# Pieces of 256 columns for POOL's subtractions, gates as scalar operands, one copy moved to VectorE, q transposed a step ahead, three idle products

## The chip, the cores and the metric

The kernel runs on one core of one Trainium2 chip. The metric is device time in microseconds (us) of one execution; the time before is the median of three runs. Beside that median stands one execution recorded by the hardware profiler, whose rows are shown below. The engines are TensorE (PE, with its weight load as PEld), VectorE (DVE), ScalarE (ACT), GpSimd (POOL) and SyncE (SP), whose queue issues the DMA transfers.

## The reference

A trunk of two layers over 256 tokens of width 1024, in f32. Cut to its core:

```
for i in range(2):
    proj = x @ w_in[i]                        # one input projection
    mix  = nsa_mixer(...) if i == 0 else mla_mixer(...)   # 12 heads of 64
    xa   = memory_cross_attention(xq, mk, mv)             # 4 heads, 256 memory tokens
    y    = concat([mix, xa]) @ w_out[i]
    x    = layer_norm(alpha * x + y)
    x    = layer_norm(alpha * x + hier_moe(x))   # top group of 4, top 2 of its 4 experts
```

The mixer of layer 0 (`nsa_mixer`) has three branches for each head, each weighted by a sigmoid gate of its own and then added:

```
o = gb[..., 0:1] * o_c + gb[..., 1:2] * o_s + gb[..., 2:3] * o_w
```

`o_c` attends to compressed keys and values (blocks of 32 tokens through a small network), `o_s` to the selected blocks of 64 tokens, `o_w` to a window of 512, which with 256 tokens is plain causal attention. 12 query heads share 4 heads of keys and values. The mixer of layer 1 is latent attention with low-rank queries and keys.

## The kernel before

**Precision.** An f32 value is kept as two rounded halves, `h` (a cast) and `l` (the value minus the cast), and a product is three matmuls: h times h, l times h, h times l. `split` (L354 to L380) does this for a weight tile that has landed in the arena of SBUF, in two halves: the cast on ACT (L369) or DVE (L371), the subtraction on POOL (L378), in some places on DVE. `piece` (L811 to L818) does the same for a quarter of the output projection (cast L815, subtraction L816).

**Stages.** Cross attention's keys and values and the projections of layer 0 come first, to about 100 us, interleaved with attention from about 50 us; its attention lasts to about 175 us, the output projection and layer norm to 195 us. The experts of layer 0 run from 200 to 411 us, in eight pairs; the attention of layer 1 to about 505 us, its experts to about 716 us. The weights stream through one queue of SP (L239). A plan lists the loads in order; `pump` issues the next one as soon as the arena has a slot for it.

**The attention of layer 0** is a list of 14 steps of two heads each: steps 0 and 1 are cross attention, 2 to 4 the selected branch of the first half of the heads, 5 to 7 its window branch, 8 to 10 and 11 to 13 the same for the second half. `attention` (L716 to L757) writes the order by hand. While step j is being finished, step j+1 has begun: its scores on PE (L647, with the causal mask at L652), then the transposes of step j's probabilities (L696), the row maxima of j+1 on DVE (L663), the exponentials on ACT (L669, their sums come out beside them), and for each head pair on DVE the copy of the transposed probabilities out of PSUM (L705) and `factors`: reciprocal of the sums (L674), times the gate (L676). `norm` multiplies the probabilities by these factors on ACT (L684). `pv` (L713) is the product with the values.

```
def factors(self, i):
    sm = self.sm[i]
    V.reciprocal(sm, sm)
    if self.gates:
        V.tensor_tensor(sm, sm, self.gates(i), op=OP.mult)
```

Work of other kinds is put between by three means: `extra(j, late)` (from L1279) runs named work at step j, `pull(FILLS[j])` takes so much from a queue of generators, and `need(name)` drains that queue up to a name. `g_qT(kp, r)` (L1046 to L1059) transposes a pair of query heads on PE (L1051), casts the two halves on ACT (L1055) and subtracts on DVE (L1058); step 8 + r reads what `g_qT(1, r)` writes, with r = 0 coming from the queue. `v_done` (L1029 to L1032) copies projected values out of PSUM on ACT (L1031); of `vw`, the window branch's, this comes within step 6's extra work. `g_sc` (L1152) is the compressed branch's scores and `g_pc` the transposes (L1176) and copies (L1177) of its probabilities (pcT). In layer 1's attention, L905 is the last step of the layer norm, L555 the low half of a transposed x.

**Banks.** PSUM is handed out in eight banks that rotate: a product into a new bank waits until the one who read that bank last is done. `warm(n)` (L481) issues n products on constants, whose result nobody reads, into a bank of its own.

Of the kernel before, what the change touches and what calls it, by code (L numbers as in the profile page):

```python
# [10 lines left out]
F32 = mybir.dt.float32  # L11
# [4 lines left out]
OP = mybir.AluOpType  # L16
# [3 lines left out]
P = 128  # L20
S = 256
D = 1024
NT = S // P
# [18 lines left out]
FILLS = [6.0, 2.0, 3.0, 3.0, 3.0, 3.0, 3.0, 3.0, 1.6, 1.6, 1.6, 0.0, 1.6, 1.6]  # L42
# [66 lines left out]
def trunk(ctx: ExitStack, tc: tile.TileContext, A, out, dbg=None, layers=2, kb=ARENA_KB):  # L109
    nc = tc.nc  # L110
    PE, V, SC, G = nc.tensor, nc.vector, nc.scalar, nc.gpsimd
# [45 lines left out]
    def spare_room(nm, side, n):  # L157
        rp = open_pool(nm, side)
        return Arena(rp.tile([P, n * UNIT], F32, name=nm), n * UNIT)

    def open_ring(l):

        spare_for[:] = [c + str(l) for c in "gud"]
        if not extra_room:
            pools["qk"].close()
        pools["ring"].close()
        spare.append(spare_room("ring", "right", 2 if extra_room else 3))
        pump()
# [83 lines left out]
    def done(*keys):  # L252
        for k in keys:
            home(k).drop(k)
        pump()
# [95 lines left out]

    splits, parts = {}, {}

    def split(key, hi=None, lo=None):  # L354

        if key in splits:
            return
        if key not in parts:
            t = get(key)
            a, n = t.shape[1], t.shape[2]  # L360
            for ring_ in (WH, WL):
                ring_.append(ring_.pop(0))
            parts[key] = (t, a) + tuple(r[0][:, :a * n].rearrange("p (a b) -> p a b", a=a) for r in (WH, WL))
        t, a, wh, wl = parts[key]
        hi, lo = hi or ((SC, SC) if key in ("kc", "vc", "vs") else (V, SC)), lo or (G, G)
        for j in range(2):
            c = slice(j * a // 2, (j + 1) * a // 2)
            if hi[j] is SC:
                SC.copy(wh[:, c, :], t[:, c, :])  # L369
            elif hi[j]:  # L370
                hi[j].tensor_copy(wh[:, c, :], t[:, c, :])  # L371
        if lo[0] is None:
            return
        for j in range(2):
            c = slice(j * a // 2, (j + 1) * a // 2)
            if lo[j] is None:
                return
            lo[j].tensor_tensor(wl[:, c, :], t[:, c, :], wh[:, c, :].bitcast(F32), op=OP.subtract)  # L378
        splits[key] = (wh, wl)
        done(key)  # L380

# [95 lines left out]
    def warm(n):  # L477

        b = bank("warm")
        for _ in range(n):  # L480
            PE.matmul(b, onesb, onesb[:, None, :].to_broadcast([P, 4, P]), start=True, stop=True)  # L481
# [57 lines left out]
    def run(g):  # L539
        for _ in g:  # L540
            pass
# [90 lines left out]
    class Step:  # L632
# [39 lines left out]
        def factors(self, i):  # L672
            sm = self.sm[i]
            V.reciprocal(sm, sm)  # L674
            if self.gates:
                V.tensor_tensor(sm, sm, self.gates(i), op=OP.mult)  # L676

        def norm(self, i):
            n0, sm = self.n0, self.sm[i]
# [33 lines left out]
                PE.matmul(o[i * 64:(i + 1) * 64, q0:S], vget(i, k), pTs[i][:, a:a + S - q0],  # L713
                          start=first and k == 0, stop=False, skip_group_check=True)

    def attention(steps, fills, extra, prologue, last=lambda: None):  # L716


        steps[0].scores()
        steps[0].softmax_a()  # L720
        for i in range(2):
            steps[0].exps(i)
        for i in range(2):
            steps[0].factors(i)
            steps[0].norm(i)
        pull(prologue)
        for j, st in enumerate(steps):
            nx = steps[j + 1] if j + 1 < len(steps) else None
            if nx is not None:
                nx.scores()  # L730
            else:
                last()
            st.transposes()
            if nx is not None:
                nx.softmax_a()
                nx.exps(0)
                if nx.act:
                    nx.exps(1)
                    for i in range(2):
                        st.evac(i, V)  # L740
                        nx.factors(i)
                    for i in range(2):
                        nx.norm(i)
                else:
                    st.evac(0, V)
                    st.evac(1, SC)
                    nx.factors(0)
                    nx.norm(0)
                    nx.exps(1)
                    nx.factors(1)  # L750
                    nx.norm(1)
            else:
                st.evac(0, V)
                st.evac(1, SC)
            extra(j, 0)
            pull(fills[j])
            st.oget(st)  # L757
            extra(j, 1)
# [51 lines left out]
    def piece(l, h, part, q, hi, lo):  # L810

        key = "wo%d_%d%s" % (l, h, part)
        t = get(key)[:, 2 * q:2 * q + 2, :]
        wh, wl = splits[key, q] = [r[:, q * 1024:(q + 1) * 1024].rearrange("p (c f) -> p c f", c=2) for r in W0]
        (hi.copy if hi is SC else hi.tensor_copy)(wh, t)  # L815
        lo.tensor_tensor(wl, t, wh.bitcast(F32), op=OP.subtract)  # L816
        if q:
            done(key)  # L818

# [114 lines left out]
    def nsa():  # L934
        tmp = ar.temp

        v_sb = {"vw": tmp("vw_sb", [P, NT, 256])}
# [90 lines left out]

        def v_done(name):  # L1029
            def f(pa):  # L1030
                SC.copy(v_sb[name], pa.rearrange("p (t c) -> p t c", t=NT))  # L1031
            return f  # L1032

        def q_done(pas):
# [12 lines left out]
        def g_qT(kp, r):  # L1047

            pt = bank()
            for t in range(NT):  # L1050
                PE.transpose(pt[:, t * P:(t + 1) * P],  # L1051
                             q_tm[:, t, 2 * r:2 * r + 2, :].rearrange("p h d -> p (h d)"), ident)
            for i in range(2):
                q, v = qS[kp][2 * r + i], pt[i * 64:(i + 1) * 64, :S]
                SC.copy(q[0:64, :], v)  # L1055
            for i in range(2):
                q, v = qS[kp][2 * r + i], pt[i * 64:(i + 1) * 64, :S]
                V.tensor_tensor(q[64:P, :], v, q[0:64, :].bitcast(F32), op=OP.subtract)  # L1058
            yield 0.21  # L1059
# [192 lines left out]
        def branch_steps(b, kp, kname, vname, first, deps):  # L1252
            res = []
            for r in range(3):
                p_ = kp * 3 + r

                def fin(s_, r=r, p_=p_):
# [16 lines left out]
        steps = (cross_steps(0, xqT, obx)  # L1274
                 + branch_steps(1, 0, "ks", "vs", True, lambda: (need("ksT", "qT0"), pull(1.3))) + branch_steps(2, 0, "kw", "vw", False, kw_ready)
                 + branch_steps(1, 1, "ks", "vs", True, lambda: need("qT1")) + branch_steps(2, 1, "kw", "vw", False, None))
# [3 lines left out]
        def extra(j, late):  # L1280
            if not late:

                if j == 1:
                    run(g_qT(0, 1))
                    run(g_qT(0, 2))
                if j == 5:
                    run(g_kT("ks", 1))
                if j == 6:
                    need("vw")
                    open_ring(0)  # L1290
                if j == 7:
                    run(g_qT(1, 1))
                if j == 8:
                    run(g_qT(1, 2))
                    ar.drop("ks_tm", "okx", "q_tm")
                    pump()
                if j == 9:
                    run(g_kT("kw", 1))
                    ar.drop("kw_tm")
                    pump()  # L1300
                if j == 11:
                    run(g_pc(1))
                    q_("pv1", g_cmp_pv(1))
                if j in (9, 10):
                    next(sc1[0])
                return
            if j == 8:
                sc1.append(g_sc(1))
            if j in (8, 9):
                next(sc1[0])  # L1310
            if 5 <= j < 5 + 4:
                next(prep)
            if j == 10:
                need("o0a")
                piece(0, 1, "a", 0, SC, G)
                piece(0, 1, "a", 1, SC, G)
                pump()
            if j == 12:
                need("pv1")
                ar.drop("vs_sb", "vblk0", "vblk1", "pcT0", "pcT1", "sc")  # L1320
                pump()
            if j == 1:
                SC.copy(okx, obx[0])
                ring_close("px", "pTx")
                ar.drop("mkT0", "mv0_sb", "xqT")
                ar.set_top(12.5)
                pump()
            if j == 6:
                need("vw")
                evac_o(okx, 6)  # L1330
            if j == 7:
                need("pv0")
                q_("o0a", g_out(0, 0))
            if j == 7:
                evac_o(ob[0], 0)
            if j == 8:
                evac_o(ob[1], 2, 1)

        pull(2.0)
        ring_open(*CROSS)  # L1340
        attention(steps, FILLS, extra, 3.0, lambda: first_pieces(0))
        need("pv1")
        evac_o(ob[2], 3)
        evac_o(ob[3], 5, 1)
# [3 lines left out]
    def first_pieces(l):  # L1348
        for t in range(NT):
            g_piece(l, 1, "a", 0, t)  # L1350
# [751 lines left out]
```

## Time and profile before

| | us |
|---|---|
| three runs | 736.11, 736.69, 737.65 |
| median | 736.69 |
| profiled execution | 737.44 |
| its span | 735.7 |
| PE busy | 702.9 (96%) |
| DVE busy | 290.5 (39%) |
| ACT busy | 217.3 (30%) |
| POOL busy | 146.6 (20%) |

The span runs from the first instruction to the last; 1.74 us of the profiled execution lie around it. Busy shares are means over stages with different limits: PE is busy nearly all the time in the experts' stages and less in the attention stages. POOL's work lies almost wholly before 200 us and in layer 1's attention.

### The profile page before, as it was taken

The numbers are of one execution on the slowest core, as the hardware profiler recorded it, in microseconds if no ns is written. First come the engines' busy times: TensorE is split into PE (matmuls) and PEld (weight loads), VectorE is DVE, ScalarE is ACT, GpSimd is POOL, SyncE is SP. The second block draws the span as 40 slices with busy tenths as digits, with TensorE's granted clock in tenths as the row PEclk, the third lists the DMA queues.
The fourth block names the chain that finished last, engine by engine and source line by source line (L and its number), as shares of the span: only waits on it lengthen the run. The fifth ranks groups of instructions, "written<-read, shape, count | busy, mean of one in ns | idle before, by whom it ended". The sixth has DMA issues, their size and how long they took to land. (4 is left out here: it accounts for less than half of the span.)

```text
span 735.7 us, 10761 instructions
## 1 busy us (share of the span) xinstructions
PE 702.9 (96%) x4119; PEld 418.9 (57%) x4119; DVE 290.5 (39%) x706; ACT 217.3 (30%) x527; POOL 146.6 (20%) x164
## 2 busy tenths in 40 slices
PE   7999998889999999999998999999999999999993
PEld 6999897767643534435344587777435335344342
DVE  4367686763640311121010767646512112111106
ACT  4454457573320301101001465443213001011011
POOL 5887444030210400000000450021203000000003
PEclk9999999789999999999999999999999999999997
DMA  9895865427698999999999995457879999999971
GB/s 294 256 281 163 302 247 175 192 72 269 233 342 329 419 352 421 419 419 418 420 419 380 385 395 212 156 223 290 343 303 420 418 419 418 421 418 419 421 264 58
DMA packets 66727, 235.57 MB, mean 320 GB/s; under 512 B 10923, under 2 KB 30446, under 8 KB 47214
## 3 DMA queue, kind: packets, MB, share of 16 engines
q1 hardware_dynamic: 66670, 234.82, 82.9%
q8 instruction: 34, 0.56, 0.3%
q14 instruction: 23, 0.19, 0.1%
HBM read 233.76 MB, written 1.05 MB: 319 GB/s over the span
## 5 line engine op out<-in xcount | busy, mean ns | idle before, releaser
L1772 PE MATMUL yb<-arena 128*64 128x512 f32 x328 | 88.7, 595 | 0.0
L378 POOL TENSOR_TENSOR wl<-arena,wh 128x1024 fp32r<-128x1024 f32 (+3 forms) x35 | 81.7, 2360 | 29.0 <-ACT wh L369 12.0
L1715 DVE SCALAR_TENSOR_TENSOR arena<-arena,csb,u 128x512 f32<-128x512 f32 x16 | 12.0, 748 | 184.1 <-PE u L1599 103.0
L898 POOL TENSOR_TENSOR lnmv<-lnmv,mhalf 128x1 f32<-128x1 f32 x8 | 6.4, 804 | 367.5 <-DVE lnmv L897 367.1
L1599 PE MATMUL g<-arena 128*64 128x512 f32 x196 | 53.8, 593 | 0.0
L1777 DVE TENSOR_TENSOR y<-yb,y 128x512 fp32r<-128x512 f32 x28 | 19.4, 691 | 85.4 <-ACT y L1776 85.4
L1772 PEld LDWEIGHTS yb<-arena 128*64 128x64 f32 x328 | 27.3, 137 | 42.1 <-issue 40.9
L1599 PE MATMUL u<-arena 128*64 128x512 f32 x180 | 49.8, 593 | 0.6 <-DMA arena<-in_moe_w_up_dram 0.6
L669 ACT ACTIVATE arena<-s,mx 128x128 f32<-128x128 f32 (+1 forms) x88 | 36.9, 429 | 37.2 <-DVE mx L663 35.9
L1776 ACT CAST y<-yb 128x512 fp32r<-128x512 f32 x28 | 16.4, 585 | 89.7 <-PE yb L1772 89.7
L1599 PE MATMUL u<-arena,xg 128*64 128x512 f32 x168 | 40.7, 593 | 1.4 <-DMA arena<-in_moe_w_up_dram 1.4
L1727 ACT COPY arena<-hT 128x256 f32<-128x256 f32 x16 | 6.0, 372 | 120.1 <-DVE arena L1727 120.1
L1599 PE MATMUL g<-arena,xg 128*64 128x512 f32 x144 | 39.7, 592 | 0.0
L1772 PE MATMUL yb<-split,arena 128*64 128x512 f32 x112 | 39.4, 596 | 0.0
L1608 PE MATMUL acc<-y,SkT 128*128 128x512 f32 (+1 forms) x136 | 38.5, 405 | 0.0
L1713 ACT ACTIVATE arena<-g 128x512 f32<-128x512 f32 x16 | 9.6, 597 | 91.2 <-PE g L1599 91.2
L1608 PEld LDWEIGHTS acc<-y,SkT 128*128 128x128 f32 x136 | 22.6, 189 | 15.8 <-issue 12.9
L663 DVE TENSOR_REDUCE mx<-s 128x1 f32<-128x128 f32 (+1 forms) x88 | 27.0, 362 | 10.1 <-PE s L652 5.5
L1599 PEld LDWEIGHTS g<-arena 128*64 128x64 f32 x196 | 16.8, 137 | 23.3 <-issue 22.4
L1599 PEld LDWEIGHTS u<-arena 128*64 128x64 f32 x180 | 15.4, 137 | 25.1 <-issue 23.6
L1599 PEld LDWEIGHTS u<-arena,xg 128*64 128x64 f32 x168 | 12.8, 137 | 24.7 <-issue 22.3
L1544 POOL TENSOR_TENSOR xl<-x_tm,xh 128x512 fp32r<-128x512 f32 x8 | 12.0, 1538 | 68.9 <-ACT xh L1543 68.9
(416 smaller groups left out, 1400.4 us busy)
## 6 DMA issues: line engine op xcount, KB each, us to landing
arena<-in_moe_w_down_dram SPq DMA_DIRECT2D x41, 1024.0 KB, 11.0
arena<-in_moe_w_up_dram SPq DMA_DIRECT2D x41, 1024.0 KB, 15.8
arena<-in_moe_w_gate_dram SPq DMA_DIRECT2D x35, 1024.0 KB, 15.7
arena<-in_moe_w_gate_dram SPq DMA_DIRECT2D x31, 512.0 KB, 6.5
split<-in_moe_w_down_dram SPq DMA_DIRECT2D x14, 1024.0 KB, 17.4
split<-in_moe_w_gate_dram SPq DMA_DIRECT2D x13, 1024.0 KB, 14.6
arena<-in_nsa_w_in_dram SPq DMA_DIRECT2D x7, 1024.0 KB, 8.0
arena<-in_moe_w_up_dram SPq DMA_DIRECT2D x14, 512.0 KB, 4.4
```

The source lines that it names most:

```text
L378: lo[j].tensor_tensor(wl[:, c, :], t[:, c, :], wh[:, c, :].bitcast(F32), op=OP.subtract)
L663: V.tensor_reduce(self.mx[i][:, t:t + 1], v, axis=AX.X, op=OP.max, negate=True)
L669: SC.activation(self.p[i][:, a:a + n], self.sb[i][:, a:a + n], AF.Exp, bias=self.mx[i][:, t:t + 1], scale=1.0, accum_out=self.sm[i][:, t:t ...
L898: G.tensor_tensor(mv[:, 3:4], mv[:, 2:3], mhalf, op=OP.pow)
L1544: G.tensor_tensor(zl, z, zh.bitcast(F32), op=OP.subtract)
L1599: PE.matmul(b_[e * 64:(e + 1) * 64, :], at[k][1](i * n + c)[:, e * 64:(e + 1) * 64], w_[e][:, c, :], start=(i + c == 0), stop=(i * n + c = ...
L1608: PE.matmul(acc[t][hf][:, a:b], SkT[k % 2][:, t * P:(t + 1) * P], yhl[hf][n][:, a:b], start=(k == 0 and n == 0), stop=(k == 7 and n == 1 a ...
L1713: SC.activation(h_sb, gp, AF.Silu)
L1715: V.scalar_tensor_tensor(h_sb, h_sb, gs[:, k % 2:k % 2 + 1], up_, op0=OP.mult, op1=OP.mult)
L1772: PE.matmul(yb[hf][e * 64:(e + 1) * 64, :], hT[:, 2 * q + c, e * 64:(e + 1) * 64], w_[e][:, c, hf * 512:(hf + 1) * 512], start=(q + c == 0 ...
L1776: SC.copy(yhl[hf][0], yb[hf])
L1777: V.tensor_tensor(yhl[hf][1], yb[hf], yhl[hf][0].bitcast(F32), op=OP.subtract)
```

## The change

Five edits, all in layer 0's part but the first, which holds for both:

1. `split` and `piece`: a subtraction on POOL is issued as instructions of 256 columns (of one row of weights where a row is 384 to 512 wide) instead of one of up to 1024. Casts, and subtractions on DVE, stay whole.
2. `factors`: the product with the gate becomes two instructions, one a column, with the gate as scalar operand.
3. `v_done`: the copy of `vw` goes from ACT to DVE.
4. `extra`: `g_qT(1, 1)` moves from step 7 to step 6, `g_qT(1, 2)` from 8 to 7.
5. `attention` takes a list `thin`; at step 12 three idle products stand between the scores of step 13 and the transposes of step 12.

The bank that `warm` takes shifts the rotation of banks after it by one.

The lines of the kernel after are four to eleven higher (L378 is L383, L676 is L682, L1031 is L1042, L1058 is L1069).

```
+    def short_pieces(eng, c):
+        return [slice(i, i + 1) for i in range(c.start, c.stop)] if eng is G else [c]
...
-            lo[j].tensor_tensor(wl[:, c, :], t[:, c, :], wh[:, c, :].bitcast(F32), op=OP.subtract)
+            for d in short_pieces(lo[j], c):
+                lo[j].tensor_tensor(wl[:, d, :], t[:, d, :], wh[:, d, :].bitcast(F32), op=OP.subtract)
...
-                V.tensor_tensor(sm, sm, self.gates(i), op=OP.mult)
+                for t in range(NT):
+                    V.tensor_scalar(sm[:, t:t + 1], sm[:, t:t + 1], self.gates(i)[:, t:t + 1], None, op0=OP.mult)
...
-    def attention(steps, fills, extra, prologue, last=lambda: None):
+    def attention(steps, fills, extra, prologue, last=lambda: None, thin=()):
...
+            if j in thin:
+                warm(3)
             st.transposes()
...
-        lo.tensor_tensor(wl, t, wh.bitcast(F32), op=OP.subtract)
+        for a in [(slice(i, i + 1), slice(j * 256, j * 256 + 256)) for i in range(2) for j in range(2)] if lo is G else \
+                [(slice(0, 2), slice(0, 512))]:
+            a = (slice(0, P),) + a
+            lo.tensor_tensor(wl[a], t[a], wh[a].bitcast(F32), op=OP.subtract)
...
-                SC.copy(v_sb[name], pa.rearrange("p (t c) -> p t c", t=NT))
+                (V.tensor_copy if name == "vw" else SC.copy)(v_sb[name], pa.rearrange("p (t c) -> p t c", t=NT))
...
                 if j == 6:
                     need("vw")
                     open_ring(0)
+                    run(g_qT(1, 1))
                 if j == 7:
-                    run(g_qT(1, 1))
+                    run(g_qT(1, 2))
                 if j == 8:
-                    run(g_qT(1, 2))
                     ar.drop("ks_tm", "okx", "q_tm")
...
-        attention(steps, FILLS, extra, 3.0, lambda: first_pieces(0))
+        attention(steps, FILLS, extra, 3.0, lambda: first_pieces(0), (12,))
```

On DVE, around the end of step 6's extra work, the kernel before has this order. `sm` are the factors, `xTh` and `xTl` the places of the transposed q, `pt` a bank of transposes, L875 a reduction for the router, L793 the low half of an attention output.

```order
L705 COPY arena<-pT 128x384
L674 RECIPROCAL sm<-sm 128x2
L676 TENSOR_TENSOR sm<-sm,arena 128x2
L1058 TENSOR_TENSOR xTh<-pt,xTh 64x256
L1058 TENSOR_TENSOR xTl<-pt,xTl 64x256
L875 TENSOR_REDUCE arena<-arena 128x20
```

The kernel after has, at the same place:

```order
L711 COPY arena<-pT 128x384
L679 RECIPROCAL sm<-sm 128x2
L682 TENSOR_SCALAR sm<-sm,arena 128x1 x2
L1042 COPY arena<-pa 128x512
L1069 TENSOR_TENSOR xTh<-pt,xTh 64x256
L1069 TENSOR_TENSOR xTl<-pt,xTl 64x256
L1069 TENSOR_TENSOR xTh<-pt,xTh 64x256
L1069 TENSOR_TENSOR xTl<-pt,xTl 64x256
L886 TENSOR_REDUCE arena<-arena 128x20
```

The copy of `vw` (L1042) now stands on DVE behind the factors; two pairs of subtractions for q follow instead of one, the pair of r = 1 first, then that of r = 0.

On ACT, before, the copy of `vw` and the casts of q r = 0 stand behind the normalisations (L684) of step 7:

```order
L684 ACTIVATE arena<-arena,sm 128x128
L684 ACTIVATE arena<-arena,sm 128x256
L1031 COPY arena<-pa 128x512
L1055 CAST xTh<-pt 64x256
L1055 CAST xTl<-pt 64x256
L792 CAST xTh<-arena 128x512
```

After:

```order
L690 ACTIVATE arena<-arena,sm 128x128
L690 ACTIVATE arena<-arena,sm 128x256
L1066 CAST xTh<-pt 64x256
L1066 CAST xTl<-pt 64x256
L1066 CAST xTh<-pt 64x256
L1066 CAST xTl<-pt 64x256
L800 CAST xTh<-arena 128x512
```

The copy is gone here, and the two casts of q r = 0 follow two of r = 1.

On PE, after, between the scores of step 13 (L652, L657) and the transposes of step 12 (L702) stand the idle products (L486); before, the transposes follow the scores directly:

```order
L652 MATMUL s_2060<-y_90,xTl 128x256 x2
L657 LDWEIGHTS identb
L657 MATMUL s_2060<-cmask,identb 128x128
L657 LDWEIGHTS identb
L657 MATMUL s_2060<-cmask,identb 128x128
L486 LDWEIGHTS onesb
L486 MATMUL warm<-onesb 128x512
L486 LDWEIGHTS onesb
L486 MATMUL warm<-onesb 128x512
L702 MATMUL pT<-ident,arena 128x128 x6
L1197 MATMUL ob_1919<-arena 64x256 x4
```

Three pairs of weight load and product come in.

## Rows read from the trace of the kernel before

**Rows 1.** The page: TensorE's granted clock in 40 slices, tenths.

```profile
PEclk9999999789999999999999999999999999999997
```

**Rows 2.** Waits of PE: waiting line, releaser; total us, times, longest.

```profile
PE ob L713 <- ACT arena L1031: 2.0, 1, 2.0
PE u L1599 <- DMA arena<-in_moe_w_up_dram: 2.0, 2, 1.4
PE pT L696 <- DVE sm L674: 1.4, 1, 1.4
PE sc L1152 <- DVE xTh L1058: 1.4, 1, 1.4
...
PE s L647 <- DVE q L1058: 1.2, 1, 1.2
PE pT L696 <- ACT arena L1177: 1.1, 2, 0.7
...
PE pt L930 <- DVE x_tm L905: 0.6, 1, 0.6
PE mi L1880 <- DVE xTl L555: 0.6, 1, 0.6
```

**Rows 3.** Windows, PE: stretch, length, busy (count), clock, DMA share, GB/s.

```profile
128.00:130.00 2.00, 2.00 (x11) 0.50 1.10 451
166.00:168.00 2.00, 2.00 (x11) 0.50 1.02 416
```

**Rows 4.** Timeline, PE in attention: start, us, instructions [idle before <-releaser].

```profile
127.88 1.55 PE L713 MATMUL ob<-arena 128*64 128x256 f32 x8 [2.02 <-ACT arena L1031]
...
150.37 0.72 PE L647 MATMUL s<-y,xTh 128*128 128x128 f32 x4
...
161.41 1.02 PE L696 MATMUL pT<-ident,arena 128*128 128x128 f32 x3 [1.43 <-DVE sm L674]
...
194.20 0.59 PE L481 MATMUL warm<-onesb 128*128 128x512 bf16 x2
```

**Rows 5.** One line, L676: ns min/median/max of 24.

```profile
L676 DVE TENSOR_TENSOR sm<-sm,arena x24: 161/161/2294, 86.9 to 164.5; 128x2 f32<-128x2 f32 x24
```

**Rows 6.** Timeline: the product of L676 and POOL's subtractions beside it.

```profile
86.89 1.81 DVE L676 TENSOR_TENSOR sm<-sm,arena 128x2 f32<-128x2 f32 x1
...
116.67 4.74 POOL L378 TENSOR_TENSOR wl<-arena,wh 128x1024 fp32r<-128x1024 f32 x2 [0.98 <-PE pT L696]
...
119.65 1.78 DVE L676 TENSOR_TENSOR sm<-sm,arena 128x2 f32<-128x2 f32 x1
...
158.49 2.29 DVE L676 TENSOR_TENSOR sm<-sm,arena 128x2 f32<-128x2 f32 x1
```

**Rows 7.** Lines by form, DVE, 0 to 190: count, busy us, mean ns.

```profile
L674 DVE RECIPROCAL sm<-sm 128x2 f32<-128x2 f32 x28 | 4.5, 162 | 2.0 <-ACT arena L669 1.6
...
L705 DVE COPY arena<-pT 128x512 f32<-128x512 f32 x4 | 2.7, 677 | 0.0
```

**Rows 8.** Lines by form, POOL, whole span.

```profile
L378 POOL TENSOR_TENSOR wl<-arena,wh 128x1024 fp32r<-128x1024 f32 x25 | 61.8, 2495 | 21.5 <-ACT wh L369 12.0 <-issue 3.0 <-DVE wh L371 2.9
L1544 POOL TENSOR_TENSOR xl<-x_tm,xh 128x512 fp32r<-128x512 f32 x8 | 12.0, 1538 | 68.9 <-ACT xh L1543 68.9
...
L378 POOL TENSOR_TENSOR wl<-arena,wh 128x768 fp32r<-128x768 f32 x4 | 7.3, 1840 | 6.9 <-PE s L652 6.9
...
L1158 POOL TENSOR_TENSOR arena<-arena,cm 128x180 f32<-128x180 f32 x2 | 1.0, 493 | 22.9 <-DVE cm L1156 22.9
```

**Rows 9.** Timeline, POOL and PE in the projections.

```profile
17.96 9.95 POOL L378 TENSOR_TENSOR wl<-arena,wh 128x1024 fp32r<-128x1024 f32 x4 [0.69 <-DVE wh L371]
...
28.60 4.81 POOL L378 TENSOR_TENSOR wl<-arena,wh 128x1024 fp32r<-128x1024 f32 x2 [0.69 <-DVE wh L371]
...
35.56 1.07 PE L570 MATMUL pa<-wl,xTh 128*128 128x256 f32 x8
...
64.50 0.73 PE L570 MATMUL pa<-wl,xTh 128*128 128x256 f32 x4 [0.23 <-POOL wl L378]
```

## The prediction

> **What bounds the kernel now.** I began with the page: TensorE's clock row and the waits of TensorE. The clock row [rows 1] shows one dip, in the eighth and ninth slices of 18.4 us (about 129 to 166 us), which is the attention of layer 0; the last slice is the end of the work. The chain that ended last covers only the final microseconds, because the program branches, so I read each stage by what TensorE waits for [rows 2]. In the two expert stages TensorE waits for 2.0 us on DMA in all, in two waits; in between it computes without a gap. So whatever TensorE gains before layer 0's experts, or in the second attention, shifts all that follows by the same amount, unless a transfer is then late (rival below).
>
> The waits that the change can touch add up to 2.0 (for the copy of vw), 1.4 (for the factors of step 12), 1.4 (for q, at the compression scores), 1.2 (for q, at 91 us), 1.1 in two waits (for the copy of pcT), and 0.6 and 0.6 in the second attention: 8.3 us [rows 2]. Behind them lies a second price. In windows of 2 us the granted clock stands at 0.50, the 1.2 GHz level, at 128 and at 166 us [rows 3]. What TensorE did just before is each time one of the long waits: 2.02 us up to 127.88, and 1.43 us up to 161.41 [rows 4]. After the 1.2 us wait at 91 us the clock row shows no dip.
>
> Why are the factors late? VectorE's product of the reciprocal with the gate, 128x2 from two operands in SBUF, takes 161 ns as a median but up to 2294 [rows 5]. The timeline [rows 6] shows what it meets. At 119.65 it takes 1.78 us and ends at 121.43; POOL's two subtractions of 128x1024 run from 116.67 for 4.74 us and end at 121.41. So the product ends when POOL's instruction ends. The same happens at 86.89 (1.81) and 158.49 (2.29). The reciprocal before it, with one operand, has a mean of 162 ns over 28 [rows 7]: it isn't held up.
>
> The Trainium skill ("SBUF — State Buffer", section "Who interferes with whom") says that the port shared by VectorE and GpSimd is held for a whole instruction, and that a VectorE instruction contends when it reads two operands from SBUF. The trace agrees: 2294 ns at the most for the product, 162 ns for the reciprocal.
>
> **The change part by part.**
>
> *Factors as scalar operand.* Each of 24 products becomes two instructions of 128x1 with one operand tile. No such instruction stands in the trace; the reciprocal of 128x2 (162 ns) is the nearest. So 0.32 us instead of 0.16, 24 times: 24 x 0.16 = 3.8 us more VectorE, spread over the attention, where VectorE is not what TensorE mostly waits for. Bounds: 0 (they pipeline) and 3.8 us on the path; I take none by itself, and 0.16 inside the two places where VectorE is late. What goes are the stalls of 1.81, 1.78 and 2.29, less 0.16 each. If such an instruction is held up too, pieces of 256 columns still cap the stall at one piece.
>
> The Trainium skill speaks against this part: "VectorE: DVE Perf Modes", section "Rules for kernel authors", wants chained VectorE work in as few instructions as possible. By that rule the 3.8 us are a loss, and the sum below would be 4.0 instead of 7.8 if all of it lay on the path. No run here shows that price.
>
> *POOL in pieces.* The POOL forms [rows 8] give a line: 128x180 takes 493 ns, 128x768 1840, so 2.29 ns a column between them, and 128x256 comes to 493 + 76 x 2.29 = 667 ns. Four are 2.67 us against 2.37 undisturbed (4.74 for two [rows 6]): 0.30 more. The bounds: 493 ns (the 180 columns; then four are 1.97, a gain) and 769 (half of the 128x512 at 1538; then 3.08, or 0.71 more). 768 columns split into two of 384: 2 x 0.96 against 1.84, a difference under 0.1 us, and I take the few other widths as even, too. With 25 of L378 and four of L816, POOL is busy 29 x 0.30 = 8.7 us longer, mostly beside TensorE's own work. There are two places without cover [rows 9]. At 64.50 TensorE waits 0.23 for the second of two subtractions in a row: 2 x 0.30 = 0.6 comes on top. From 17.96 four run in a row for 9.95 us, and two more from 28.60 to 33.41. TensorE comes to the last half of these in the middle of its eight products from 35.56, near 36.1. Six times 0.30 is 1.8; POOL idles 0.7 before 28.60, so the last piece comes 1.1 later, against 2.7 of slack. VectorE's casts may slip in between pieces now, so I take 0.2. Cost 0.8, bounds -0.4 to 2.5.
>
> *At 86 to 92 us.* The product at 86.89 no longer stands for 1.81, so ScalarE's normalisation, its casts of q and VectorE's subtractions come about 1.6 earlier: the wait of 1.2 goes but for 0.1. Gain 1.1, bounds 0.5 to 1.2.
>
> *At 118 to 151 us.* Without the stall at 119.65 the copy of pcT is in time; that wait is 0.7 of the 1.1. The wait of 2.0 for the copy of vw at 127.88 [rows 4] goes from ScalarE, where the copy stood behind four normalisations; on VectorE it stands behind the factors of step 7 only. With q transposed a step ahead the 1.4 at the compression scores goes. These make 4.1. New: the copy on VectorE itself, 0.68 (as the 128x512 from PSUM [rows 7]), and q r=0, which the order now puts behind q r=1 on both engines (two casts, two subtractions). Its pair of subtractions is two instructions of 64x256, which cost no more than the 128x512 copies at 0.68 and no less than 0.16 each; I take 0.8 for the pair. So 4.1 - 0.7 - 0.8 = 2.6. This takes the clock as it is. If the clock stays up through 128 to 134 us, TensorE runs there in half the time, but then waits for ScalarE and VectorE, whose work to the scores at 150.37 doesn't shrink; I put 1.0 more on it, so 3.6 at most. Bounds 0 (the new waits eat it all) to 3.6.
>
> *At 155 to 174 us.* Product stall of 2.29 gone, the factor is there before TensorE wants it, and the wait of 1.43 at 161.41 goes. But the three idle products shift the rotation of the PSUM banks by one: the first transpose now needs the bank of pcT, which ScalarE empties after the normalisation. Today the second half of the transposes waits for that same copy, for 0.4 of the 1.1 [rows 2], so the copy ends near 161.41 + 1.02 + 0.4 = 162.8. It comes 2.1 earlier with the stall gone, at 160.7; I take 161.0, so the transposes start only 0.4 earlier. What else changes is the clock: TensorE has three products (0.59 for two [rows 4], so 0.9 in all) in what was its longest gap here, so its idle time here falls under the 1.2 that did nothing at 91 us. From 161.4 to about 168.3 (the window at 166 is wholly at the lower level) it ran at the lower level; the same products at the higher one take half of 6.9, so 3.4 is won. Together 3.8, felt by all that follows. Bounds: 0.4 + 0.9 = 1.3 (the clock falls all the same, and only part of the wait is won) to 4.2.
>
> *Second attention.* The two waits of 0.6 follow a VectorE instruction with two SBUF operands that overlaps a subtraction of POOL (832 and 1024 columns). With pieces at most 416 wide the hold-up is at most a third to a half: 1.1 won, bounds 0.4 to 1.2.
>
> **The sum.** 1.1 + 2.6 + 3.8 + 1.1 - 0.8 = 7.8. The profiled execution took 737.44 us (span 735.7 and 1.74 around it), so 729.6; the runs' median, 736.69, lies 0.75 below it, so 728.9. My main case runs from 726.5 to 731.5.
>
> **Rivals.**
>
> *The gain is partly given back.* The clock falls anyway at 128 and 166 us, because new waits (the q order, the bank of pcT) are long enough. Then the 155-174 term is 1.3 and the 118-151 term some 1.0: 1.1 + 1.0 + 1.3 + 1.1 - 0.8 = 3.7, so 733.0 (732 to 735.2). For it: the clock fell after 1.43 us already. Against it: at 91 us 1.2 did nothing.
>
> *Everything lands.* The clock stays up in all three places and no new wait is felt: 1.2 + 3.6 + 4.2 + 1.2 + 0.4 = 10.6, so 726.1 or a little less. Against it: the q order adds a wait for certain.
>
> *Nothing measurable.* Measurement of this kernel tells about 0.2% (1.5 us) from no change. The gain may be lost further on: the expert stages already wait 2.0 on DMA, and weights for the first of them arrive when slots come free. If the attention ends 7.8 earlier and the first experts' weights do not, TensorE waits there instead: 735.2 to 738.2. Against it: in the trace those two waits hold only 2.0 us in all, and the queue of loads waits for slots that TensorE itself frees, so the loads move too.
>
> *Slower: POOL becomes the bound of the projections.* If a piece of 256 costs far more than the line says, because of a start cost with every instruction, POOL sets the pace from 18 to 36 us and at 64 us. At 1.1 us a piece four are 4.4, so 2.03 more each: six in the first stretch are 12.2, less the 0.7 and 2.7 of slack, so 8.8, and two at 64.50 are 4.1: 12.9 lost against 8.6 won, 4.3 more than 736.69, so 741.0. It decides from about 1.0 a piece: 8 x 1.63 - 3.4 = 9.6, which is 1.0 over what is won. Against it: the 180 columns took 493 ns, so a start cost of 0.5 can't hide there.
>
> **How the numbers follow.** Main case 0.50, given back 0.25, everything 0.10, nothing measurable 0.08, slower 0.07. Predicted: 728.9. The range of 8 in 10 leaves out the better half of the best case and the two last: 725.0 to 735.5. Faster by over 0.2% (below 735.2) 0.85, within 0.2% 0.08, slower 0.07.
>
> **What would show it.** The two-instruction factors have a mean near 0.16 each and a maximum no longer than one piece of POOL. The 256-column piece has a mean of 0.65 to 0.70. In the list of waits the entries for the copy of vw, the factors of step 12 and the compression scores are gone or under 0.5; a wait for q at the scores of step 8 is new. The windows at 166 us show a granted clock of 1.00, those at 128 and 146 us may not. The first product of the experts starts some 6 to 7 us earlier. The prediction is wrong if the pieces cost over 0.8, if the clock at 160 to 168 stays at 0.50, or if the experts start earlier and the end doesn't move with them.

## The result and the profile after

The kernel after takes 727.30 us (median of four executions, 726.37 to 728.83) against 737.17 for the kernel before (four, 736.11 to 737.79): a ratio of 0.987, 95% interval 0.9846 to 0.9894, so 9.9 us faster. Forecast were 728.9 and a range of 725.0 to 735.5. The profiled execution took 728.83 us, the slowest of the four; its span is 727.0 against 735.7.

First the factors, one line of the kernel after: ns as minimum, median and maximum of 48.

```profile
L682 DVE TENSOR_SCALAR sm<-sm,arena x48: 202/208/215, 88.6 to 159.1; 128x1 f32<-128x1 f32 x48
```

None of the 48 is held up; the product of before took up to 2294 ns [rows 5]. Each takes 208 ns where 160 was forecast; the two of a pair overlap and take 0.34 together, where 0.32 was. Beside them in the timeline stand POOL's pieces, still at work while the factors pass:

```profile
116.50 3.79 POOL L383 TENSOR_TENSOR wl<-arena,wh 128x512 fp32r<-128x512 f32 x3 [0.97 <-PE s L657]
...
118.14 0.34 DVE L682 TENSOR_SCALAR sm<-sm,arena 128x1 f32<-128x1 f32 x2
...
119.05 0.34 DVE L682 TENSOR_SCALAR sm<-sm,arena 128x1 f32<-128x1 f32 x2
```

The waits of TensorE (the views of [rows 2]): the entries for the copy of vw, the factors and the compression scores are gone. New or longer are those for the transposed probabilities (L711), for q at step 8's scores (L1069), for k at step 11's (L1033), and two more for POOL.

```profile
PE ob L719 <- DVE arena L711: 1.8, 3, 1.1
PE s L652 <- DVE xTh L1069: 1.3, 1, 1.3
...
PE s L652 <- ACT y L1033: 0.9, 1, 0.9
PE pa L575 <- POOL wl L383: 0.8, 3, 0.3
```

The products of [rows 4] in the timeline after:

```profile
125.22 0.87 PE L719 MATMUL ob<-arena 128*64 128x256 f32 x8
127.38 0.72 PE L652 MATMUL s<-y,xTh 128*128 128x128 f32 x4 [1.28 <-DVE xTh L1069]
...
144.14 0.33 PE L652 MATMUL s<-y,xTh 128*128 128x128 f32 x1 [0.88 <-ACT y L1033]
144.87 0.61 PE L652 MATMUL s<-y,xTh 128*128 128x128 f32 x3 [0.41 <-DVE y L1036]
...
155.83 0.81 PE L486 MATMUL warm<-onesb 128*128 128x512 bf16 x3
156.83 0.87 PE L702 MATMUL pT<-ident,arena 128*128 128x128 f32 x6 [0.19 <-ACT arena L1188]
```

Step 11's scores start at 144.14 instead of 150.37, the transposes of step 12 at 156.83 instead of 161.41, the first product of the experts at 191.33 instead of 199.59. The clock stands at 1.00 at 128 and 166 us, where [rows 3] have 0.50; but a dip of some 3 us has come at 146 (columns as in [rows 3]):

```profile
128.00:130.00 2.00, 1.74 (x17) 1.00 1.03 424
...
146.00:148.00 2.00, 2.00 (x12) 0.50 0.04 8
148.00:149.00 1.00, 1.00 (x4) 0.50 0.02 8
...
156.00:160.00 4.00, 3.81 (x30) 1.00 0.60 201
...
166.00:168.00 2.00, 2.00 (x10) 1.00 1.03 403
```

No wait of the old length stands before it, only those of 0.88 and 0.41 us. Of the price of POOL's pieces two views speak, the forms on POOL (count, busy us, mean ns) and the timeline of TensorE in the projections, where [rows 9] have one wait of 0.23:

```profile
L383 POOL TENSOR_TENSOR wl<-arena,wh 128x256 fp32r<-128x256 f32 x84 | 63.5, 795 | 12.6 <-ACT wh L373 7.2 <-PE pa L610 3.0 <-issue 2.4
...
L827 POOL TENSOR_TENSOR wl<-arena,wh 128x256 fp32r<-128x256 f32 x16 | 11.1, 733 | 29.9 <-ACT wh L823 29.9
```

```profile
18.05 0.38 PE L575 MATMUL pa<-wl,xTh 128*128 128x256 f32 x1 [0.23 <-POOL wl L383]
18.74 0.39 PE L575 MATMUL pa<-wl,xTh 128*128 128x256 f32 x1 [0.30 <-POOL wl L383]
...
66.31 0.39 PE L575 MATMUL pa<-wl,xTh 128*128 128x256 f32 x1 [0.30 <-POOL wl L383]
```

A piece costs 733 to 795 ns, not 667, just under the 0.8 us that the prediction named as a sign of being wrong; four are 2.9 to 3.2 us.

To compare executions that start at slightly different times, I take stretches between the same products in each timeline: from the first product of the projections (near 9 us) to the selected branch's first scores (near 84, "projections"); on to step 7's scores (near 120); on to step 11's; on to the first product of the experts; and in layer 1 from the first to the last product of its input projection. Times in us; a stretch in which the clock fell for some us is marked.

| kernel | median | projections | to step 7 | 7 to 11 | 11 to experts | layer 1 |
|---|---|---|---|---|---|---|
| before | 737.17 | 75.2 | 36.8 | 29.7 (dips) | 49.2 (dip) | 13.1 |
| after | 727.30 | 76.7 | 35.1 | 23.5 | 47.2 (dip) | 12.1 |
| whole subtractions | 726.66 | 75.6 | 35.1 | 23.5 (dip) | 45.6 | 13.1 |
| product of two tiles | 727.69 | 76.8 | 35.2 | 24.5 | 45.6 | 12.1 |
| no idle products | 726.21 | 76.2 | 35.1 | 23.5 | 45.3 | 12.1 |
| q late | 731.14 | 76.9 | 35.1 | 26.1 | 45.6 | 12.1 |
| scalar operand alone | 730.02 | 76.4 | 35.1 | 26.6 | 45.3 | 13.1 |
| pieces alone | 732.01 | 77.7 | 35.2 | 28.4 (dips) | 44.6 | 12.1 |
| copy on ScalarE | 727.56 | 77.3 | 35.1 | 24.0 (dip) | 45.7 | 12.1 |
| q order | 726.74 | 76.7 | 35.1 | 23.5 | 45.3 | 12.2 |
| after again | 726.95 | 77.5 | 35.1 | 23.5 | 47.2 (dip) | 12.1 |
| pieces in layer 1 only | 725.63 | 75.3 | 35.1 | 23.5 | 45.3 | 12.2 |
| k early (whole in layer 0) | 726.56 | 77.2 | 35.1 | 24.1 | 44.6 | 12.1 |
| idle at 7 (whole in layer 0) | 726.69 | 75.4 | 35.1 | 25.7 (dip) | 44.7 | 12.2 |

The stretches are of the one profiled execution, the medians of all. The experts take the time between them unchanged: from their first product to the idle products ahead of layer 1 it is 212.7 us before and 213.0 after, so what the attention gains reaches the end.

### The profile page after: what moved, and what is told of

Its sections match the earlier page's. It is cut to its first block, busy times and chain, and to the rows that moved or that the text cites. A ratio compares the mean times of both kernels' runs of the same rounds, so it can differ in the third digit from the quotient of the medians.

```text
span 727.0 us, 10956 instructions
## 1 busy us (share of the span) xinstructions
PE 697.5 (96%) x4122; PEld 414.7 (57%) x4122; DVE 281.7 (39%) x731; ACT 217.3 (30%) x526; POOL 162.0 (22%) x253
## 5 line engine op out<-in xcount | busy, mean ns | idle before, releaser
L383 POOL TENSOR_TENSOR wl<-arena,wh 128x256 fp32r<-128x256 f32 (+4 forms) x112 | 95.3, 889 | 21.0 <-ACT wh L373 7.2
L1555 POOL TENSOR_TENSOR xl<-x_tm,xh 128x512 fp32r<-128x512 f32 x8 | 12.1, 1542 | 68.9 <-ACT xh L1554 68.9
```

Of the source, the lines that this page charges most:

```text
L383: lo[j].tensor_tensor(wl[:, d, :], t[:, d, :], wh[:, d, :].bitcast(F32), op=OP.subtract)
L1555: G.tensor_tensor(zl, z, zh.bitcast(F32), op=OP.subtract)
```

## The experiments

**Whole subtractions, or the product again: is it the pieces or the scalar operand that frees the factors?** The first undoes the pieces, the second the scalar operand, each in the kernel after.

```
-        return [slice(i, i + 1) for i in range(c.start, c.stop)] if eng is G else [c]
+        return [c]
```

> The kernel after with POOL's subtractions whole again (up to 1024 columns), all else kept. Theory A (the scalar operand alone frees the factors, pieces only cost): the factor instructions stay near 0.21 us, TensorE's waits on POOL before 70 us go (about 1.4 us won), the two waits in layer 1's attention come back (1.0 us lost): 0 to 1 us faster than the kernel after, about 727. Theory B (the pieces are what lets VectorE in): factors of up to 2.3 us come back, and the wait before the transposes of step 12 with its clock dip: 3 to 6 us slower, 730 to 733.

Measured: 726.66 us (726.27 to 728.10), ratio to before 0.9855 (0.9834 to 0.9876). The line of the factors and TensorE's waits in layer 1:

```profile
L682 DVE TENSOR_SCALAR sm<-sm,arena x48: 202/209/216, 87.1 to 156.0; 128x1 f32<-128x1 f32 x48
```

```profile
PE mi L1890 <- DVE xTl L560: 0.6, 1, 0.6
```

Even beside whole subtractions of 2.4 us no factor is held up: theory A. The 0.6 in layer 1 is back.

```
-                for t in range(NT):
-                    V.tensor_scalar(sm[:, t:t + 1], sm[:, t:t + 1], self.gates(i)[:, t:t + 1], None, op0=OP.mult)
+                V.tensor_tensor(sm, sm, self.gates(i), op=OP.mult)
```

> The kernel after with the factors as one product of two SBUF operands again (128x2), pieces of 256 kept. Theory A (the scalar operand is what counts): the product is held up by up to one piece at five or so places; with pieces of 0.75 us that is 0.6 each, and behind the pieces in a row maybe longer: the wait before step 12's transposes grows again, 2 to 5 us slower, 729 to 732. Theory B (the pieces count): hold-ups of at most 0.75 us that other work hides; 0 to 1 us slower or even a little faster, since 24 instructions fewer run: 726.5 to 728.

Measured: 727.69 us (727.31 to 728.09), ratio 0.9862 (0.9843 to 0.9881).

```profile
L681 DVE TENSOR_TENSOR sm<-sm,arena x24: 161/162/898, 88.8 to 158.5; 128x2 f32<-128x2 f32 x24
```

The hold-up now ends with one piece, at 898 ns instead of 2294, and with it steps 7 to 11 take 1.0 us more (24.5 against 23.5). That is theory B here: short pieces do for the factors nearly what the scalar operand does. The scalar operand alone frees them wholly, the pieces alone cut the hold-up to at most the rest of one piece.

**Each of them alone, on the kernel before.** The edits are those of the diff.

> The kernel before with the gates as scalar operands alone. Theory A (either the scalar operand or the pieces free the factors; the rest of the gain is the order of q and of the copy of vw): factors all near 0.21 us, the waits at 91 us (1.2), on the copy of pcT (0.7) and for the factors of step 12 (1.4) go, the waits for the copy of vw (2.0) and at the compression scores (1.4) stay at 1 us or more: 3 to 6 us faster than the kernel before, depending on where the clock falls. Theory B (the scalar operand carries nearly all): 8 to 10 us faster.

Measured: 730.02 us (729.89 to 733.22), ratio 0.9914 (0.9881 to 0.9948): 7.6 faster. Waits of TensorE:

```profile
PE sc L1153 <- DVE xTh L1059: 1.5, 1, 1.5
...
PE ob L714 <- ACT arena L1032: 1.0, 1, 1.0
```

The factors take 202 to 215 ns. The wait for the copy of vw halves by itself, that at the compression scores stays, as theory A has it; the gain is between the two theories' sums.

> The kernel before with POOL's subtractions in pieces alone. Theory A: the product is held up by at most 0.9 us, the same waits go as with the scalar operand, layer 1's attention gains 1.0, the projections lose 1.5: 2.5 to 5.5 us faster than the kernel before. Theory B (pieces cost and do nothing more): 1.5 us slower to 1 us faster.

Measured: 732.01 us (731.09 to 732.78), ratio 0.9926 (0.9900 to 0.9953): 5.6 faster, just over theory A's upper end. The product takes 904 ns at the most. But the copy's wait stays at 2.0 and the clock still dips twice:

```profile
PE ob L718 <- ACT arena L1039: 2.0, 1, 2.0
```

```profile
128.00:132.00 4.00, 3.60 (x24) 0.73 1.04 422
144.00:148.00 4.00, 4.00 (x23) 0.64 0.23 98
```

7.6 and 5.6 are not two gains to be added: the two edits act on the same hold-up.

**No idle products.** The argument `(12,)` is dropped.

> The kernel after without the three idle products at step 12, all else kept. Theory A (they keep TensorE's clock up from 156 to 163 us): the idle time before the transposes is about 1 us instead of 0.2, the granted clock falls to 0.50 after it, and the 6 us that follow take 3 us longer: 2 to 3.5 us slower, 729.5 to 731. Theory B (the wait is short already without the stall of the factors, and the clock would stay up by itself): within 0.4 us of the kernel after, 727.

Measured: 726.21 us (725.83 to 726.40), ratio 0.9841 (0.9825 to 0.9858). TensorE around its transposes, and its windows there:

```profile
153.78 0.50 PE L702 MATMUL pT<-ident,arena 128*128 128x128 f32 x3
154.78 0.55 PE L702 MATMUL pT<-ident,arena 128*128 128x128 f32 x3 [0.50 <-ACT arena L1188]
```

```profile
152.00:156.00 4.00, 3.18 (x28) 1.00 0.01 2
156.00:160.00 4.00, 4.00 (x28) 1.00 0.78 283
```

Theory A is wrong: without the products the clock stays at 1.00, and step 11 to the experts takes 45.3 us, where the versions with the products and without a dip take 45.6 or 45.7. The idle products win nothing here and cost 0.3, because they push the transposes behind the copy of pcT as a whole, where without them the first half runs ahead of it.

**q late.** `g_qT(1, 1)` and `(1, 2)` back at steps 7 and 8.

> The kernel after with q transposed where it was (r = 1 at step 7, r = 2 at step 8), all else kept. Theory A (having q ahead removes the wait at the compression scores and with it a clock dip): the wait of 1.3 us at step 8's scores goes, one of about 1.4 us at the compression scores comes, and the clock falls behind it: 1 to 4 us slower, 728.5 to 731. Theory B (the order only moves a wait from one place to another of the same size): within 0.5 us, 727.

Measured: 731.14 us (730.24 to 731.37), ratio 0.9909 (0.9892 to 0.9925): 3.8 slower than the kernel after.

```profile
126.75 0.72 PE L652 MATMUL s<-y,xTh 128*128 128x128 f32 x4 [0.39 <-DVE xTh L1069]
133.61 0.73 PE L652 MATMUL s<-y,xTh 128*128 128x128 f32 x4 [1.09 <-DVE xTh L1069]
139.66 0.28 PE L1163 MATMUL sc<-kcS,xTh 128*128 128x32 f32 x1 [1.49 <-DVE xTh L1069]
140.21 0.25 PE L1163 MATMUL sc<-kcS,xTl 128*128 128x32 f32 x1 [0.27 <-DVE xTl L1069]
```

Late q is waited for four times, 3.24 us in all; ahead it is waited for once, 1.28. Between steps 7 and 11 this is worth 2.6 us (26.1 against 23.5), and up to step 11's scores the clock stays at 1.00 in both profiled executions, so it isn't the reason for these 2.6: theory A by its waits, not by its dip. The rest of the 3.8 I don't place: the four other executions of this kernel have a lower mean clock (0.989) than the profiled one (0.994) and take 0.5 to 1.1 us more than its 730.24, so a dip in them is possible and not shown.

**The copy of vw on ScalarE.**

> The kernel after with the copy of vw on ScalarE again. Theory A (behind four normalisations it is late even without the stall of the factors): TensorE waits about 1.2 us for it at 125 us instead of 0.3, but the scores of step 8 then wait less for q: 0.5 to 1.5 us slower than the kernel after, 728 to 729. Theory B (the next wait takes it all up): within 0.4 us, 727.

Measured: 727.56 us (727.25 to 728.78), ratio 0.9870 (0.9843 to 0.9897). TensorE waits 0.8 for the copy and 1.1 for q, and steps 7 to 11 take 0.5 longer (24.0), in an execution whose clock fell there. The medians differ by 0.3 and the ratios to the kernel before not at all (0.9870 both): in the time it is theory B.

**q r = 0 ahead of r = 1** (and no idle products).

```
                     open_ring(0)
+                    need("qT1")
                     run(g_qT(1, 1))
```

> The kernel after without the idle products, and with q r = 0 cast and subtracted ahead of r = 1 at step 6 (both still a step ahead). Theory A (the new wait of 1.3 us at step 8's scores is the place of r = 0 behind r = 1, and costs): that wait falls to about 0.4; TensorE is then earlier by 0.9, of which the wait for the copy of the transposed probabilities right behind it gives back a part: 0.3 to 0.9 us faster than the kernel without idle products, 725.3 to 726. Theory B (VectorE and ScalarE set the pace there, the wait only moves): no difference, 726.2.

Measured: 726.74 us (725.52 to 728.45), ratio 0.9861 (0.9830 to 0.9891).

```profile
125.92 0.72 PE L652 MATMUL s<-y,xTh 128*128 128x128 f32 x4 [0.39 <-DVE xTh L1069]
130.31 1.91 PE L719 MATMUL ob<-arena 128*64 128x256 f32 x16 [2.02 <-DVE arena L711]
```

```profile
128.00:132.00 4.00, 1.98 (x19) 1.00 0.98 391
```

Step 8's scores start 0.9 earlier, and 0.9 more is then waited for the copy of the transposed probabilities (2.02 instead of 1.13): theory B. VectorE and ScalarE set the pace there. And after 2.02 us of waiting, the same wait as in [rows 4], the clock stays at 1.00.

**The kernel after again, and three further versions.**

> The kernel after as it is, for the comparison with the three that follow. 727.3 as before, in two levels 2 us apart (about 726.4 and 728.5). Theory A (the upper level is a clock dip behind the wait at step 11's scores): executions of the upper level have the lower mean clock or a stretch at 0.50 in the trace, those of the lower level none. Theory B (the levels come from the first loads): no relation to the clock.

Measured: 726.95 us, five executions: 726.76, 726.83 and 726.95 with a mean granted clock of 0.994, and 729.81 and 730.12 with 0.992 and 0.990. The profiled one is the last; its window and a wait in its first loads:

```profile
148.00:152.00 4.00, 4.00 (x16) 0.60 0.01 2
```

```profile
PE pa L610 <- DVE wh L375: 1.5, 1, 1.5
```

Both theories hold a part: the dip makes step 11 to the experts 47.2 instead of 45.6, so 1.6 us, and the start another 1 to 2. In these five the upper level has the lower mean clock. In the first four executions of this kernel it has not: 726.37 and 726.50 came with 0.991, 728.10 with 0.993 and 728.83 with 0.992. So the clock alone doesn't sort the two levels.

> The kernel after without the idle products and with pieces of 256 in layer 1's attention only; layer 0's subtractions are whole. Theory A (in layer 0 the pieces are superfluous beside the scalar operand and cost 1.2 to 1.5 us in the projections, in layer 1 they win 1.0): 724.7 to 725.3, 1 to 1.5 us faster than without idle products alone. Theory B (start-up scatter is larger than what the pieces cost): 726.2, no difference.

Its pieces are bound to the keys of layer 1's weights; layer 0 is whole but for its output projection, and there are no idle products. Measured: 725.63 us (724.88 to 728.80), ratio 0.9845 (0.9818 to 0.9872) beside 0.9863 (0.9837 to 0.9889) for the kernel after on the same chip. Projections 75.3, layer 1 12.2: by its stretches it has the good part of each, theory A, and its median is the lowest of all. But that median is 0.6 below the one without idle products, whose ratio to the kernel before is 0.9841, so the times don't decide between the theories; and the next version, with the same subtractions, has 77.2 in the projections. That it beats the kernel after is likely and not shown, since the intervals overlap.

> As the one with pieces in layer 1 only, and the window branch's keys of the second half (cast and subtraction of k) evacuated at step 8 instead of 9. Theory A (the waits of 0.9 and 0.4 at step 11's scores are for these): both go, 0.8 to 1.3 us faster than without, 723.5 to 724.5. Theory B (ScalarE's and VectorE's chain of step 10 is then late by the same amount): no difference.

This kernel writes k of the second half over keys that steps 8 to 10 still read, so it computes other scores; its instructions and their sizes are the same. Measured: 726.56 us (724.73 to 728.56), ratio 0.9849 (0.9822 to 0.9876). Step 9 to 10 takes 6.5 us instead of 5.1, and steps 10 to 12 as much less: theory B.

> As the one with k early, and three idle products ahead of step 8's scores, where TensorE waits 1.3 us for q. Theory A (they fill a wait that lets the clock fall now and then, and cost nothing since TensorE waits there anyway): the executions lie closer together, none with a stretch at 0.50 near 128 us, median equal to or up to 1 us under the same kernel without them. Theory B (the clock's falls don't hang on this wait, or the products delay the scores): equal or 0.3 to 0.8 us slower.

With k as in the one before. Measured: 726.69 us (725.09 to 726.80), ratio 0.9845 (0.9822 to 0.9868). The wait at step 8's scores shrinks to 0.53, and the clock dips elsewhere:

```profile
140.00:144.00 4.00, 4.00 (x16) 0.64 0.00 0
```

Theory B in the time and the clock. The executions do lie closer together than those of the one before (1.7 us from lowest to highest against 3.8), as theory A has it; five of each are too few to tell.

## Why the prediction was right, and where it wasn't

The forecast of 728.9 missed the measured 727.3 by 1.6, and by the profiled executions 7.8 was forecast and 8.6 came. The sum is closer than its terms, and that is luck: one term was 3.6 too small, and a dip of 1.6 us and a start 0.7 dearer than forecast took 2.3 of that back in the profiled execution.

*The hold-up by POOL* was read rightly, and shown: without the second SBUF tile no factor is held up, and without the long subtraction none for longer than 904 ns. The prediction gave both edits as one cause and kept "a piece caps the stall" as a reserve; it did not say that either alone would do most of it. It priced three hold-ups; the trace of before has two more, of 1.23 us at 102.03 and 0.76 at 118.31. One thing no run separates: the edit also narrows the instruction from 128x2 to 128x1. For the operand speaks the reciprocal, which reads one tile of the same 128x2 and was never held up in the kernel before:

```profile
L674 DVE RECIPROCAL sm<-sm x44: 149/166/168, 51.4 to 483.6; 128x2 f32<-128x2 f32 x44
```

*86 to 92 us*: forecast 1.1. The stretch to step 7 lost 1.6 to 1.7 in every version (36.8 to 35.1), 0.6 more than forecast. The wait for q was the only one that I counted there, and it goes wholly (1.17). Up to the scores that waited for it the kernel after is 1.4 faster (7.7 to 6.3 us), and a wait of 0.18 at 118.18 goes as well; the rest I didn't separate.

*118 to 151 us* is the step that failed in size: forecast 2.6, at most 3.6, measured 6.2 (29.7 to 23.5). Cut at the same four products of each trace (the one that waited for vw, step 9's scores, the compression product that waited for q, step 11's scores), the stretch is, in us:

| kernel | to vw's product | to step 9's scores | to the compression | to step 11's scores |
|---|---|---|---|---|
| before | 7.2 | 8.4 (dip) | 6.0 | 8.1 (dip) |
| pieces alone | 6.5 | 7.9 (dip) | 6.0 | 8.1 (dip) |
| scalar operand alone | 5.2 | 8.0 | 6.0 | 7.4 |
| q late | 4.6 | 8.1 | 6.0 | 7.4 |
| after | 4.6 | 7.7 | 4.2 | 7.0 |

The term that was wrong is q. I counted one wait for it, the 1.4 at the compression scores, and charged a new one of 0.8, so 0.6 was to be won. Late q is waited for oftener than that, in the kernel before at 136.29 and 142.82 too, and once more where the wait for vw hides it:

```profile
136.29 0.72 PE L647 MATMUL s<-y,xTh 128*128 128x128 f32 x4 [0.43 <-DVE xTh L1058]
...
142.27 0.28 PE L1152 MATMUL sc<-kcS,xTh 128*128 128x32 f32 x1 [1.41 <-DVE xTh L1058]
142.82 0.25 PE L1152 MATMUL sc<-kcS,xTl 128*128 128x32 f32 x1 [0.27 <-DVE xTl L1058]
```

Being ahead wins 2.6 net (q late against after). Ahead of vw's product 2.6 came where 2.0 was forecast (0.7 for pcT and 2.0 for vw, less 0.7 for the copy); some 0.5 of it is the copy's place (scalar operand alone against q late, both without a dip; these two differ in the pieces too). The clock's part, which I left out of the sum and held to 1.0 at most, is about 0.7, all in the last column: there pieces alone, with a dip, takes as long as before, and the scalar operand alone, without one, 0.7 less, though it waits 0.86 for k there. In the second column pieces alone has a dip and is no slower than the scalar operand alone without one, so there no cost of the clock is to be seen. That VectorE and ScalarE cap what the clock gives back was therefore right. These make 2.6 + 2.6 + 0.7 = 5.9 of the 6.2; the rest is in small differences of the second column.

*155 to 174 us*: forecast 3.8. From step 12's scores to the first product of the experts it is 43.84 us before and 39.58 after, so 4.3 won. (From step 11's scores on it is 3.6 where no dip came, 49.2 to 45.6, mainly because step 11's scores now wait 0.4 for k in their midst.) The size is right and the reason half wrong. It is the clock, but the idle products don't keep it up: without them it stays at 1.00 and the stretch is 0.3 shorter. That the stall went was enough; either edit alone, without idle products, has 39.3 there. In the profiled execution the dip at 146 takes 1.6 back, so only 2.0 of the 3.6 are seen there.

*Layer 1*: forecast 1.1; measured 1.0 (13.1 to 12.1) in every version with pieces there, and none in those without. In the kernel after 0.4 of it goes again just ahead of this stretch (the last lines of this document).

*The price of the pieces*: forecast 0.8 for the projections. Eight profiled executions with pieces take 76.2 to 77.7 there (mean 77.0), six with whole subtractions 75.2 to 77.2 (mean 75.8): 1.1, with a scatter as large as itself. The piece was mis-sized, at 667 ns by a line through other forms; it takes 733 to 795. POOL did not become the bound, as the slower rival had it.

*The rival "everything lands"* at 726.1 is closest to the lower executions of the kernel after (726.4 to 727.0); their traces weren't taken.

The Trainium skill's rule to keep chained VectorE work in few instructions ("VectorE: DVE Perf Modes", section "Rules for kernel authors") speaks against this change, and the prediction took it to cost 3.8 if all of it lay on the path. The trace shows what it costs: the 48 keep VectorE busy for 8.0 us, against 24 x 0.162 = 3.9 without a hold-up, so 4.1 more; but with the hold-ups the 24 took 11.1. In the kernel after the only wait for the 48 is one of 0.4 us of TensorE's weight load. So the rule's price is real, lies off the path here, and is less than the hold-ups that it buys off.

## What to carry to other kernels

Where an engine's instruction varies by ten times, look whose instruction ends when it ends; then look at both sides of the hold-up: one alone may do most of it, so choose the side whose cost lies off the path. Count every wait for a late operand, small ones too, before you price an order. And a chance clock dip can take 1.6 us of such a kernel and its start another 1 to 2: judge changes of 1 us by several executions and by stretches of the trace, not by one span.

## What was not expected of the hardware

The dips of TensorE's clock are not bound to a wait of a given length, nor to one place. A wait of 2.02 us left it at 1.00 (q order); in the kernel after it fell behind waits of 0.88 and 0.41, and behind waits of 0.86 and 0.41 at the same scores it stayed at 1.00 (scalar operand alone). It fell at 126 us in one version's execution and at 146 or 148 in another's. The dip at 126 (whole subtractions) cost nothing: steps 7 to 11 take 23.5 with it and without it, and the wait for the copy of the transposed probabilities (1.13 in the kernel after) is gone in its place:

```profile
124.00:128.00 4.00, 2.72 (x21) 0.78 1.04 422
128.00:132.00 4.00, 4.00 (x32) 0.79 0.68 236
```

The Trainium skill ("TensorE: Matmul & The Clock Gate", section "Part 1: The HAM clock gate (the "warmup" mystery)") says that when the clock changes differs from run to run of the same kernel. The runs agree: the mean granted clock of the nine executions of the kernel before beside the last versions runs from 0.981 (738.97 us) to 0.988 (736.64), that of the kernel after's nine from 0.990 to 0.994. Both traces of the kernel after, at 728.83 and 730.12 us, have a dip near 146 to 151 us.

Open: in the versions built on the kernel after, TensorE waits 0.4 us more at the head of layer 1 for the layer norm; with the product of two tiles it doesn't, nor with either edit alone on the kernel before. The traces show where it arises: VectorE's last statistics for that layer norm start together with TensorE's idle products at the end of the experts (404.38 beside 404.37 us), and with the product of two tiles 0.36 ahead of them (403.43 beside 403.79). I found no reason for that.
